# Moving a data-dependent branch forward in a mixture-of-experts block, and loading half of the last down weights by rows

## The chip, the cores and the metric

The kernel runs on one core of a Trainium2 chip. The metric is the device time in microseconds of one execution, as the median of several runs. The core has a matrix engine (TensorE, PE in the rows; its weight loads are PEld), a vector engine (VectorE, DVE), an activation engine (ScalarE, ACT), GpSimd (POOL) and SyncE (SP), which here issues nearly all DMA transfers. Each engine works through its own queue in order.

## The reference

One transformer block over 256 tokens of width 2048, in float32: RMS norm, an input projection, eight heads of a gated delta rule and eight heads of block attention, an output projection, and then a hierarchical mixture of experts with a final RMS norm. The part around the change is this one:

```python
def hierarchical_moe(x, w_rg, b_rg, w_re, b_re, w_gate, w_up, w_down):
    # 4 groups of 8 experts; each token takes the best group and the two best experts in it
    ...
    expert_id = g_idx * EXPERTS_PER_GROUP + e_idx
    y = grouped_expert_ffn(xf, expert_id, w_gate, w_up, w_down)
    out = jnp.einsum('nk,nkd->nd', gates, y.astype(jnp.float32))

# per expert, on the tokens sent to it:
#   h = silu(x @ w_gate[e]) * (x @ w_up[e]);  y = h @ w_down[e]

def reference(...):
    ...
        x = x + hierarchical_moe(h, ...)
    return rmsnorm(x, norm_final_w)
```

There are 32 experts; gate and up weights are 2048 x 512, down weights 512 x 2048, all float32, so an expert has 12.6 MB.

## The kernel before, in words

**Slots.** Every expert gets 64 slots for tokens. Experts are worked in groups of four (`quad(g, last)`, g = 0 to 7, called quads in the code), and a group in two pairs (`pr`). A pair's two experts stand side by side in the 128 partitions, 64 slots each. `one_hots` makes the tile `oh` that says which token goes to which slot; `gather` multiplies the tokens (split into a high and a low part, `xh` and `xl`) by it on TensorE into `ph`, and VectorE turns that into `hT`. `hidden` multiplies `hT` by gate and up weights (`pgate`, `pup`, 2048 rows in two halves). ScalarE and VectorE form `hg`, TensorE transposes it (`pht`) to `hgT`, and the down products go to `py`. `split_y` splits those into a high and a low part on ScalarE and VectorE (`yh`, `yl`), and `combine` adds them to the tokens: two matmuls for each half of the tokens (`pcm`) and an add on VectorE into `acc`.

**Overfull experts.** When an expert gets more than 64 tokens, `overflow` works through all tokens for it in a loop. The number of such experts is known on the device only, so there is a branch: `tc.If(n < 1)` runs the rest of the groups, and its other side runs `overflow` and then the same rest. Nothing inside the branch can be interleaved with what is outside. Before, the branch stands ahead of the last group; group 7's tokens are gathered behind it, while those of groups 1 to 6 are gathered by the group ahead.

**Loads.** `quad_loads(g)` is the list of a group's weight loads, and SP runs through these lists ahead of the other engines, held only by the ring of slots (`wslot`: nine slots of 2 MB, named `wx`, `we`, `wm`). `fetch` loads a pair's block with contiguous runs per partition. The down weights of groups 0 to 6 come by rows (256 rows of all 2048 columns at a time). Those of the last group come by columns: `LASTS` lists the blocks (pair, first column, columns), most of 512 columns for a pair of experts, in four DMA pieces each, with runs of 2 KB (1 KB for the last two).

**The tail.** In the last group the order is written out by hand (`manual_schedule`). For each block of `LASTS` TensorE makes the products (`pyl`), ScalarE and VectorE split them, and the block before is combined. `norm_part` squares the sums on ScalarE as columns become final (those of the second pair), the first 1024 columns are multiplied by the final weights `fnb` on VectorE ahead of time, and after the last column the norm's factor `rf` is worked out, the outputs are scaled and five stores go out.

Of the kernel before, what the change touches and what calls it, by code (L numbers as in the profile page):

```python
# [12 lines left out]
AF = mybir.ActivationFunctionType  # L13
# [15 lines left out]
NX, NA = 2, 5  # L29
FIRST = "x" * NX + "a" * NA + "mrm"  # L30
ROUND = "x" * NX + "a" * NA + "mm"
NQ = NE // 4
PFI, PF0 = 3, 1
XA, XB = 2, 4
WARM = (7, 2, 2)
HT = 4

LASTS = ((0, 0, 512), (1, 0, 512), (0, 512, 512), (1, 512, 512), (0, 1024, 512), (1, 1024, 512), (0, 1536, 512),
         (1, 1536, 256), (1, 1792, 256))
BS = 128 * 128 + 128  # L40


# [5 lines left out]
def tile_block(ctx, tc, x, norm_mix_w, w_in, conv_w, A_log, dt_bias, gonw, monw, w_out, nfw,  # L48
# [868 lines left out]
    def next_kind():  # L917
        used[0] += 1
        return next(kind_from(used[0] - 1))

    def wslot(kind):

        if kind == "r":
            return raw_tiles(4)
        if kind == "x":
            if len(wx["x"]) < 2 * NX:
                ts = [xtp.tile([128, 2048], F32, name="wx", tag="xw", bufs=2 * NX) for _ in range(2)]
            else:
                ts = wx["x"][-2 * NX:][:2]
            wx["x"] += ts  # L930
        elif kind == "a":
            if len(wx["e"]) < NA:
                ts = [wx["a"].tile([128, 4096], F32, name="we", tag="we", bufs=NA)]
            else:
                ts = wx["e"][-NA:][:1]
            wx["e"] += ts
        else:
            ts = [wxm.tile([128, 4096], F32, name="wm", tag="wm", bufs=2)]
        return [t.rearrange("p (k c) -> p k c", c=512) for t in ts]
# [23 lines left out]
    def quad_loads(g):  # L963

        es = range(4 * g, 4 * g + 4)
        for half in range(2):
            for w in (w_g, w_u):
                for es2 in (es[:2], es[2:]):
                    yield from fetch([w[0, e, half * 1024:(half + 1) * 1024, :].rearrange("(p k) c -> p k c", k=8)
                                      for e in es2])  # L970
        if g == NQ - 1:
            rooms = {}
            for pr, c0, n in LASTS:
                if c0 % 1024 == 0:
                    ks = [next_kind() for _ in range(2)]
                    yield ks[0]
                    rooms[pr] = [wslot(k) for k in ks]

                vs = [[t.rearrange("p k c -> p (k c)").rearrange("p (f c) -> p f c", c=1024)[:, :, c0 % 1024:c0 % 1024 + n]
                       for t in ts] for ts in rooms[pr]]  # L980
                rows = [[v[f // (4 // len(v))][:, f % (4 // len(v)):][:, 0:2] for f in (0, 2)] for v in vs]
                for i in range(2):
                    for j in range(2):
                        src = w_d[0, es[2 * pr + j], i * 256:(i + 1) * 256, c0:c0 + n]
                        nc.sync.dma_start(rows[j][i], src.rearrange("(f p) c -> p f c", p=128))
                yield [[r[f // 2][:, f % 2] for f in range(4)] for r in rows]
            return
        for es2 in (es[:2], es[2:]):
            for half in range(2):
                yield from fetch([w_d[0, e, half * 256:(half + 1) * 256, :]  # L990
                                  .rearrange("(p k) c -> p k c", k=2).rearrange("p k (i c) -> p (k i) c", c=512)
                                  for e in es2])

    gen = [0, quad_loads(0)]
    asked = [next(gen[1])]
# [13 lines left out]
    def weights():  # L1009

        while not ready:
            load_step()
        return ready.pop(0)
# [269 lines left out]
    def quad(g, last):  # L1283
# [34 lines left out]
        for pr in range(2):  # L1318
            hg = ep.tile([128, 512], F32, name="hg")
            nc.scalar.activation(hg, pgu[pr][0], AF.Silu, scale=sl[pr][:, 0:1])  # L1320
            nc.vector.scalar_tensor_tensor(hg, pgu[pr][1], sl[pr][:, 0:1], hg, op0=OP.mult, op1=OP.mult)  # L1321
            pht = ps_tmp("pht")
            for f in range(4):
                f0 = f // 2 * 256 + f % 2
                nc.tensor.transpose(pht[:, f * 128:(f + 1) * 128],
                                    hg[:, f * 128:f * 128 + 128] if last else hg[:, f0:f0 + 255:2], ident)
            hgT.append(ep.tile([128, 4, 128], F32, name="hgT", bufs=2))
            nc.scalar.copy(hgT[pr].rearrange("p f s -> p (f s)"), pht)  # L1328
        if not last and g < NQ - 2:
            noh = one_hots(g + 1)  # L1330
            nhT = [gather(noh, 0, h) for h in range(4)]
        if g == 0:
# [17 lines left out]
                if then:  # L1350
                    then(b, c0, n, pc)

        for pr in range(0 if last else 2):
            py = [ps_proj(f"py{c}") for c in range(4)]
            for f in range(4):
                if f % 2 == 0:
                    ws = weights()
                for c in range(4):
                    for j in range(2):
                        nc.tensor.matmul(py[c][j * SL:(j + 1) * SL], hgT[pr][:, f, j * SL:(j + 1) * SL],  # L1360
                                         ws[j][f % 2 * 4 + c], start=(f == 0), stop=(f == 3))
            for c in range(4):
                combine(pr, c * 512, 512, split_y(pr, 512, py[c]))
        if not last:
            if g < NQ - 2:
                start.append((noh, nhT, None))
            return

# [4 lines left out]
            nc.gpsimd.partition_broadcast(fnb[c], fnb[c][0:1], channels=128)  # L1373
        fixed = ExitStack()
        fixed.enter_context(tc.manual_schedule())
        parts_ = [(pr, c0 + o, min(n, 512), o) for pr, c0, n in LASTS for o in range(0, n, 512)]
        sums = [p for p in parts_ if p[0]]
        sf = cst.tile([128, 2, len(sums)], F32, name="sf")
        rf = cst.tile([128, 2], F32, name="rf")
        pre_ = cst.tile([128, 2], F32, name="pre_")  # L1380
        fn = lambda c0, n: fnb[c0 // 512][:, c0 % 512:c0 % 512 + n]
        late_cols = [p[1] for p in sums[-2:]]

        def norm_part(b, c0, n, pc):
            i = [p[1] for p in sums].index(c0)
            if b and c0 == late_cols[-1]:
                nc.vector.scalar_tensor_tensor(pc[:, 0:n], acc(b, c0, n), 1.0, acc(b, c0, n), op0=OP.mult, op1=OP.mult,
                                               accum_out=sf[:, b, i:i + 1])
            else:
                nc.scalar.activation(pc[:, 0:n], acc(b, c0, n), AF.Square, accum_out=sf[:, b, i:i + 1])  # L1390
                if c0 == late_cols[-1]:
                    nc.vector.scalar_tensor_tensor(pre_, sf[:, :, i - 1], 1.0 / D, pre_, op0=OP.mult, op1=OP.add)
            if c0 not in late_cols:
                if c0 < 1024:
                    muls.append((acc(b, c0, n), fn(c0, n)))

        held, muls = None, []
        for pr, c0, n, o in parts_:
            old = len(muls)
            if o == 0:  # L1400
                ws = weights()
            py = ps_proj("pyl")
            for f in range(4):
                for j in range(2):
                    nc.tensor.matmul(py[j * SL:(j + 1) * SL, 0:n], hgT[pr][:, f, j * SL:(j + 1) * SL], ws[j][f][:, o:o + n],  # L1405
                                     start=(f == 0), stop=(f == 3))
            if c0 == late_cols[-1]:
                y = ep.tile([128, 512], F32, name="hg")[:, 0:n]
                nc.scalar.activation(y, py[:, 0:n], AF.Copy, scale=sl[pr][:, 1:2])
                ys = (y,)  # L1410

                nc.vector.reduce_sum(pre_, sf[:, :, 0:len(sums) - 2], axis=AX.X)
                nc.vector.tensor_scalar(pre_, pre_, 1.0 / D, EPS, op0=OP.mult, op1=OP.add)
            else:
                ys = split_y(pr, n, py)
            if held:
                combine(*held)

            for _ in range(old):
                a, f = muls.pop(0)  # L1420
                nc.vector.tensor_mul(a, a, f)
            held = (pr, c0, n, ys, norm_part if pr else None)
        combine(*held)
        assert not muls
        ov_ = out.rearrange("o (b p) d -> (o p) b d", p=128)
        for b in range(2):
# [16 lines left out]
                nc.sync.dma_start(ov_[:, b, qs[0] * 512:qs[0] * 512 + n], a)  # L1443
        fixed.close()

    def last_quad(noh):
        start.append((noh, [gather(noh, 0, h) for h in range(4)], None))
        quad(NQ - 1, True)

    for g in range(NQ - 1):  # L1450
        quad(g, False)

    noh = one_hots(NQ - 1)
    n = nc.values_load(novi, min_val=0, max_val=7)
    seen = used[0], len(wx["x"]), list(gen), len(wx["e"])
    with tc.If(n < 1) as some:
        last_quad(noh)
    with some.Else():
        used[0], gen[:] = seen[0], seen[2]
        del wx["x"][seen[1]:]  # L1460
        del wx["e"][seen[3]:]
        overflow(n, noh)
        asked[0] = None
        last_quad(noh)


# [28 lines left out]
```

## Time and profile before

| what | value |
|---|---|
| median of 3 runs | 1430.91 us (1430.38 to 1435.44) |
| profiled execution, its own time | 1437.39 us |
| span of the profile | 1435.7 us |
| TensorE matmul busy | 1386.0 us (97%) |
| VectorE busy | 619.1 us (43%) |
| ScalarE busy | 417.0 us (29%) |
| read from device memory | 484.98 MB, 341 GB/s over the span |

A busy TensorE in this profile is not TensorE at its peak, since ends of matmuls are modelled. Each float32 matmul stands there as two instructions. The profiled execution is 6.5 us above the median of the runs.

### The profile page before, as it was taken

How to read it: one execution, taken by the hardware profiler on the slowest of the kernel's cores; microseconds unless marked ns; L12 is line 12 of the kernel's file. 1: busy time of each engine (PE TensorE's matmuls, PEld its weight loads, DVE VectorE, ACT ScalarE, POOL GpSimd, SP SyncE). 2: the span in 40 equal slices, each digit the busy share in tenths (PEclk: the TensorE clock that was granted, in tenths of full speed). 3: DMA queues.
4: the chain of work that ended last, by engine and by line, in shares of the span. 5: the costliest groups of instructions: out<-in, count | busy, mean ns of one | idle time of the engine just before them, and what ended most of it. 6: DMA issues, size and time to landing. Idle time of an engine off the chain costs nothing.

```text
span 1435.7 us, 19018 instructions
## 1 busy us (share of the span) xinstructions
PE 1386.0 (97%) x7482; PEld 815.7 (57%) x7482; DVE 619.1 (43%) x1301; ACT 417.0 (29%) x801; POOL 48.3 (3%) x84
## 2 busy tenths in 40 slices
PE   8999999999999999999999999999999899899996
PEld 8988999998888743443443443433443244235333
DVE  6876967686655541341331341241142033125014
ACT  5565436555654321120120120121121012013012
POOL 2020003000000000000000000000000000000010
PEclk9999989999999999999999999999999999999998
DMA  8667736755499689999999999999999999999996
GB/s 244 180 187 213 207 107 179 191 147 179 150 354 375 236 306 411 425 425 427 425 418 425 427 428 425 427 426 426 428 426 426 427 424 428 426 427 426 426 395 232
DMA packets 107455, 490.24 MB, mean 341 GB/s; under 512 B 23024, under 2 KB 31280, under 8 KB 78816
## 3 DMA queue, kind: packets, MB, share of 16 engines
q1 hardware_dynamic: 107056, 488.76, 87.4%
q8 instruction: 61, 1.00, 0.3%
q0 software_dynamic: 304, 0.20, 0.1%
q14 instruction: 34, 0.28, 0.1%
HBM read 484.98 MB, written 3.95 MB: 341 GB/s over the span
## 4 chain that ended last, share of the span: by engine, by line
PE 80%; DMA 10%; DVE 5%; ACT 3%; issue 1%; POOL 0%; DVEq 0%; SPq 0%; ACTq 0%
PE py L1360 15%; PE pup L1094 12%; PE pgate L1094 12%; PE pj L235 6%; PE pj L239 5%; PE pj L236 5%; DMA we<-in_w_expert_up_dram 4%; PE pj L247 4%; PE pj L248 4%; PE pj L250 4%; PE pcm L1347 3%; PE ph L1083 3%; PE pyl L1405 2%; DMA wm<-in_w_expert_up_dram 2%; DMA we<-in_w_expert_down_dram 2%; DVE acc L1349 2%
## 5 line engine op out<-in xcount | busy, mean ns | idle before, releaser
L216 DVE TENSOR_TENSOR w_lo<-w_raw,w_hi 128x512 fp32r<-128x512 f32 x288 | 193.0, 689 | 97.9 <-ACT w_hi L213 97.3
L213 ACT CAST w_hi<-w_raw 128x512 fp32r<-128x512 f32 x288 | 170.9, 619 | 84.7 <-PE pj L236 32.7
L1094 PE MATMUL pup<-we,hT 128*64 128x512 f32 x608 | 163.7, 599 | 7.7 <-DMA we<-in_w_expert_up_dram 7.6
L235 PE MATMUL pj<-xth,w_hi 128*128 128x256 f32 x640 | 168.1, 295 | 0.0
L236 PE MATMUL pj<-xtl,w_hi 128*128 128x256 f32 x640 | 161.0, 284 | 0.0
L1094 PE MATMUL pgate<-we,hT 128*64 128x512 f32 x528 | 149.3, 595 | 0.2 <-DMA we<-in_w_expert_gate_dram 0.2
L1360 PE MATMUL py<-we,hgT 128*64 128x512 f32 x480 | 144.5, 597 | 1.1 <-ACT hgT L1328 0.7
L235 PEld LDWEIGHTS pj<-xth,w_hi 128*128 128x128 f32 x640 | 122.8, 192 | 2.0 <-ACT w_hi L213 0.4
L236 PEld LDWEIGHTS pj<-xtl,w_hi 128*128 128x128 f32 x640 | 123.0, 192 | 0.3
L1072 DVE TENSOR_TENSOR hT<-ph,nfe 128x512 f32<-128x512 f32 x64 | 44.1, 688 | 169.6 <-PE pup L1094 131.7
L1321 DVE SCALAR_TENSOR_TENSOR hg<-pup,sl,hg 128x512 f32<-128x512 f32 x16 | 12.0, 751 | 231.5 <-PE pup L1094 223.6
L1338 DVE SCALAR_TENSOR_TENSOR yl<-py,sl,yh 128x512 fp32r<-128x512 f32 x56 | 40.3, 745 | 157.8 <-ACT yh L1337 156.7
L1094 PEld LDWEIGHTS pup<-we,hT 128*64 128x64 f32 x608 | 53.2, 138 | 96.7 <-issue 85.5
L1337 ACT ACTIVATE yh<-py,sl 128x512 fp32r<-128x512 f32 x56 | 37.7, 687 | 238.0 <-PE py L1360 211.9
L239 PE MATMUL pj<-xth,w_lo 128*128 128x256 f32 x640 | 103.3, 284 | 0.0
L1022 ACT CAST xh<-xs 128x512 fp32r<-128x512 f32 x64 | 73.7, 1184 | 94.3 <-PE ph L1083 64.0
L1023 DVE TENSOR_TENSOR xl<-xs,xh 128x512 fp32r<-128x512 f32 x64 | 70.6, 1118 | 47.7 <-PE ph L1083 28.7
L1094 PEld LDWEIGHTS pgate<-we,hT 128*64 128x64 f32 x528 | 45.4, 137 | 79.7 <-issue 76.2
L239 PEld LDWEIGHTS pj<-xth,w_lo 128*128 128x128 f32 x640 | 88.6, 192 | 0.0
L1349 DVE TENSOR_TENSOR acc<-acc,pcm 128x512 f32<-128x512 f32 (+1 forms) x122 | 75.4, 673 | 22.9 <-PE pcm L1347 22.8
L1360 PEld LDWEIGHTS py<-we,hgT 128*64 128x64 f32 x480 | 45.9, 136 | 66.8 <-issue 63.6
L1094 PE MATMUL pgate<-wm,hT 128*64 128x512 f32 x256 | 81.1, 595 | 0.0
(344 smaller groups left out, 1997.1 us busy)
## 6 DMA issues: line engine op xcount, KB each, us to landing
we<-in_w_expert_up_dram SPq DMA_DIRECT2D x36, 2048.0 KB, 26.9
we<-in_w_expert_gate_dram SPq DMA_DIRECT2D x33, 2048.0 KB, 24.0
we<-in_w_expert_down_dram SPq DMA_DIRECT2D x30, 2048.0 KB, 29.3
w_raw<-in_w_in_dram SPq DMA_DIRECT2D x111, 512.0 KB, 4.1
wm<-in_w_expert_gate_dram SPq DMA_DIRECT2D x16, 2048.0 KB, 28.7
wx<-in_w_expert_down_dram SPq DMA_DIRECT2D x28, 1024.0 KB, 29.4
wx<-in_w_expert_up_dram SPq DMA_DIRECT2D x28, 1024.0 KB, 26.1
wx<-in_w_expert_gate_dram SPq DMA_DIRECT2D x24, 1024.0 KB, 25.9
```

The lines of the kernel that those rows point to most:

```text
L213: nc.scalar.copy(hi, raws[n])
L216: nc.vector.tensor_sub(lo, raws.pop(n), hi.bitcast(F32))
L235: nc.tensor.matmul(o, wh[:, cs], xh[k], start=(k == 0 and c % 2 == 0), stop=False, skip_group_check=True)
L236: nc.tensor.matmul(o, wh[:, cs], xl[k], start=False, stop=False, skip_group_check=True)
L239: nc.tensor.matmul(o, wl[:, cs], xh[k], start=False, stop=(k == NK - 1), skip_group_check=True)
L247: nc.tensor.matmul(pb[b], ah[:, bs], wh, start=(k == 0), stop=False)
L248: nc.tensor.matmul(pb[b], al[:, bs], wh, start=False, stop=False)
L1022: nc.scalar.copy(hi, src)
L1023: low = lambda: nc.vector.tensor_sub(lo, src, hi.bitcast(F32))
L1094: nc.tensor.matmul(pgu[j * SL:(j + 1) * SL], hT[:, i, c0:c0 + SL], ws[j][kk], start=(half + kk == 0), stop=(half == 1 and kk == 7))
L1349: nc.vector.tensor_add(acc(b, c0, n), acc(b, c0, n) if g + pr else xs[:, b, c0:c0 + n], pc[:, 0:n])
L1360: nc.tensor.matmul(py[c][j * SL:(j + 1) * SL], hgT[pr][:, f, j * SL:(j + 1) * SL], ws[j][f % 2 * 4 + c], start=(f == 0), stop=(f == 3))
```

## The change

The branch moves from ahead of group 7 to ahead of group 4 (`BRANCH = 4`): groups 0 to 3 stand before it, groups 4 to 7 inside. The tile `oh` of the first group inside is made inside. Groups 5, 6 and 7 are gathered by the group ahead; group 4 is gathered behind the branch. In the last group the first pair's down weights are loaded by rows, as in the groups ahead, and only the second pair's by columns, in blocks of 1024, 512, 256 and 256. The hand-written order of the tail changes with it: `down(0)` makes all products of the first pair, and the products, splits and combines of the second pair's five column parts (`products`, `rows`, `add`; parts 0 to 4) are interleaved with the first pair's combines.

```diff
-NQ = NE // 4
+NQ, BRANCH = NE // 4, 4
-LASTS = ((0, 0, 512), (1, 0, 512), (0, 512, 512), (1, 512, 512), (0, 1024, 512), (1, 1024, 512), (0, 1536, 512),
-         (1, 1536, 256), (1, 1792, 256))
+LASTS = ((0, 1024), (1024, 512), (1536, 256), (1792, 256))
...
-        for es2 in (es[:2], es[2:]):
+        for es2 in (es[:2], es[2:])[:1 if g == NQ - 1 else 2]:
             for half in range(2):
                 yield from fetch([w_d[0, e, half * 256:(half + 1) * 256, :]
                                   .rearrange("(p k) c -> p k c", k=2).rearrange("p k (i c) -> p (k i) c", c=512)
                                   for e in es2])
+        if g == NQ - 1:
+            for c0, n in LASTS:
+                if c0 % 1024 == 0:
+                    ks = [next_kind() for _ in range(2)]
+                    yield ks[0]
+                    rooms = [wslot(k) for k in ks]
...
+                        src = w_d[0, es[2 + j], i * 256:(i + 1) * 256, c0:c0 + n]
+                        nc.sync.dma_start(rows[j][i], src.rearrange("(f p) c -> p f c", p=128))
...
-        if not last and g < NQ - 2:
+        if not last and g != BRANCH - 1:
             noh = one_hots(g + 1)
             nhT = [gather(noh, 0, h) for h in range(4)]
...
+        def products(i):
+            c0, n, o = sums[i]
             if o == 0:
-                ws = weights()
-            py = ps_proj("pyl")
+                blk[0] = weights()
+            pys[i] = ps_proj("pyl") if i else ps_tmp("pyl")
             for f in range(4):
                 for j in range(2):
...
+        py = down(0)
+        for i in range(2):
+            products(i)
+            ys = [split_y(0, 512, py[c]) for c in (2 * i, 2 * i + 1)]
+            for c in range(2):
+                combine(0, (2 * i + c) * 512, 512, ys[c])
+        rows(0)
+        products(2)
+        rows(1)
+        add(0)
+        rows(2)
+        products(3)
+        add(1)
+        add(2)
+        rows(3)
+        products(4)
+        rows(4)
+        add(3)
+        add(4)
...
-    def last_quad(noh):
+    def rest(noh):
         start.append((noh, [gather(noh, 0, h) for h in range(4)], None))
-        quad(NQ - 1, True)
-
-    for g in range(NQ - 1):
+        for g in range(BRANCH, NQ):
+            quad(g, g == NQ - 1)
+
+    for g in range(BRANCH):
         quad(g, False)
 
-    noh = one_hots(NQ - 1)
     n = nc.values_load(novi, min_val=0, max_val=7)
     seen = used[0], len(wx["x"]), list(gen), len(wx["e"])
     with tc.If(n < 1) as some:
-        last_quad(noh)
+        rest(one_hots(BRANCH))
     with some.Else():
...
+        noh = one_hots(BRANCH)
         overflow(n, noh)
         asked[0] = None
-        last_quad(noh)
+        rest(noh)
```

## Rows read from the trace of the kernel before

**Rows 1.** The page's 40 slices of 35.9 us: GB/s moved by DMA.
```profile
GB/s 244 180 187 213 207 107 179 191 147 179 150 354 375 236 306 411 425 425 427 425 418 425 427 428 425 427 426 426 428 426 426 427 424 428 426 427 426 426 395 232
```

**Rows 2.** Windows: us, busy PE, PEld, DVE, ACT, POOL; granted clock, DMA share, GB/s.
```profile
1248.00:1250.00 2.00, 2.00 (x6) 0.48 (x6) 0.00 (x0) 0.00 (x0) 0.00 (x0) 0.50 1.00 426
...
1310.00:1320.00 10.00, 8.20 (x44) 6.69 (x43) 9.47 (x12) 6.00 (x6) 0.00 (x0) 0.83 1.00 418
...
1314.00:1316.00 2.00, 2.00 (x12) 2.00 (x12) 2.00 (x3) 1.44 (x2) 0.00 (x0) 0.58 0.96 401
```

**Rows 3.** Timeline of TensorE: start, us, instructions, [idle before and what ended it].
```profile
1247.71 8.60 PE L1094 MATMUL pup<-we,hT 128*64 128x512 f32 x32 [3.84 <-DMA we<-in_w_expert_up_dram]
...
1309.44 0.72 PE L1083 MATMUL ph<-oh,xh 128*128 128x256 f32 x4 [0.28 <-issue]
1311.83 0.89 PE L1083 MATMUL ph<-oh,xl 128*128 128x256 f32 x4 [1.66 <-DVE xl L1023]
...
1323.41 2.79 PE L1094 MATMUL pgate<-we,hT 128*64 128x512 f32 x12
```

**Rows 4.** Timeline of SP's queue: start of an issue, its us, what it loads.
```profile
1329.68 0.33 SPq L960 DMA_DIRECT2D we<-in_w_expert_gate_dram  x1
...
1350.66 0.42 SPq L960 DMA_DIRECT2D wx<-in_w_expert_up_dram  x1
...
1413.77 0.37 SPq L985 DMA_DIRECT2D wx<-in_w_expert_down_dram  x1
```

**Rows 5.** DMA issues in windows around those three: KB, us from issue to landing.
```profile
we<-in_w_expert_gate_dram SPq DMA_DIRECT2D x1, 2048.0 KB, 17.6
...
wx<-in_w_expert_up_dram SPq DMA_DIRECT2D x1, 1024.0 KB, 26.2
...
wx<-in_w_expert_down_dram SPq DMA_DIRECT2D x1, 256.0 KB, 5.8
```

**Rows 6.** DMA packets in 1320 to 1345 us and in 1380 to 1385 us.
```profile
DMA packets 818, 10.70 MB, mean 428 GB/s; under 512 B 88, under 2 KB 88, under 8 KB 88
...
DMA packets 1054, 1.91 MB, mean 382 GB/s; under 512 B 123, under 2 KB 123, under 8 KB 1054
```

**Rows 7.** The chain that ended last, in order of time: start, us, what.
```profile
1316.55 1.21 PE ph L1083 x8
...
1366.41 6.92 PE pup L1094 x32
...
1383.46 6.20 PE pyl L1405 x26
...
1395.03 1.13 PE pcm L1347 x4
...
1411.81 3.92 PE pyl L1405 x16
...
1419.82 1.88 PE pyl L1405 x16
```

**Rows 8.** Timeline of TensorE's weight loads: the longest wait for a DMA after 1383 us.
```profile
1387.73 0.20 PEld L1405 LDWEIGHTS pyl<-we,hgT 128*64 128x64 f32 x4 [0.71 <-DMA we<-in_w_expert_down_dram]
```

**Rows 9.** Timeline of VectorE and of ScalarE in the tail.
```profile
1413.36 1.29 DVE L1421 TENSOR_TENSOR acc<-acc,fnb 128x512 f32<-128x512 f32 x2
...
1416.55 0.75 DVE L1338 SCALAR_TENSOR_TENSOR yl<-pyl,sl,yh 128x512 fp32r<-128x512 f32 x1 [1.90 <-ACT yh L1337]
1417.22 1.27 DVE L1349 TENSOR_TENSOR acc<-acc,pcm 128x512 f32<-128x512 f32 x2
...
1419.72 0.48 DVE L1338 SCALAR_TENSOR_TENSOR yl<-pyl,sl,yh 128x256 fp32r<-128x256 f32 x1 [1.23 <-ACT yh L1337]
...
1423.70 0.41 DVE L1349 TENSOR_TENSOR acc<-acc,pcm 128x256 f32<-128x256 f32 x1
...
1417.99 0.60 ACT L1390 ACTIVATE pcm<-acc 128x512 f32<-128x512 f32 x1 [1.47 <-DVE acc L1349]
...
1419.23 0.45 ACT L1337 ACTIVATE yh<-pyl,sl 128x256 fp32r<-128x256 f32 x1
```

More of the change, by code (lines that the diff above doesn't have):

```diff
@@ L970, in quad_loads @@
                                       for e in es2])
[L971 to L987, printed above, removed]
-        for es2 in (es[:2], es[2:]):
+        for es2 in (es[:2], es[2:])[:1 if g == NQ - 1 else 2]:
             for half in range(2):
@@ L992, in quad_loads @@
                                   for e in es2])
+        if g == NQ - 1:
[4 more added lines that the diff above has]
+                    rooms = [wslot(k) for k in ks]
+                vs = [[t.rearrange("p k c -> p (k c)").rearrange("p (f c) -> p f c", c=1024)[:, :, c0 % 1024:c0 % 1024 + n]
+                       for t in ts] for ts in rooms]
+                rows = [[v[f // (4 // len(v))][:, f % (4 // len(v)):][:, 0:2] for f in (0, 2)] for v in vs]
+                for i in range(2):
+                    for j in range(2):
+                        src = w_d[0, es[2 + j], i * 256:(i + 1) * 256, c0:c0 + n]
+                        nc.sync.dma_start(rows[j][i], src.rearrange("(f p) c -> p f c", p=128))
+                yield [[r[f // 2][:, f % 2] for f in range(4)] for r in rows]
     gen = [0, quad_loads(0)]
@@ L1325, in quad @@
                 nc.tensor.transpose(pht[:, f * 128:(f + 1) * 128],
-                                    hg[:, f * 128:f * 128 + 128] if last else hg[:, f0:f0 + 255:2], ident)
+                                    hg[:, f * 128:f * 128 + 128] if last and pr else hg[:, f0:f0 + 255:2], ident)
             hgT.append(ep.tile([128, 4, 128], F32, name="hgT", bufs=2))
             nc.scalar.copy(hgT[pr].rearrange("p f s -> p (f s)"), pht)
-        if not last and g < NQ - 2:
+        if not last and g != BRANCH - 1:
             noh = one_hots(g + 1)
@@ L1351, in combine, with down @@
                     then(b, c0, n, pc)
-        for pr in range(0 if last else 2):
+        def down(pr):
             py = [ps_proj(f"py{c}") for c in range(4)]
@@ L1361, in quad @@
                                          ws[j][f % 2 * 4 + c], start=(f == 0), stop=(f == 3))
-            for c in range(4):
-                combine(pr, c * 512, 512, split_y(pr, 512, py[c]))
+            return py
         if not last:
-            if g < NQ - 2:
+            for pr in range(2):
+                py = down(pr)
+                for c in range(4):
+                    combine(pr, c * 512, 512, split_y(pr, 512, py[c]))
+            if g != BRANCH - 1:
                 start.append((noh, nhT, None))
@@ L1375, in quad @@
         fixed.enter_context(tc.manual_schedule())
-        parts_ = [(pr, c0 + o, min(n, 512), o) for pr, c0, n in LASTS for o in range(0, n, 512)]
-        sums = [p for p in parts_ if p[0]]
+        sums = [(c0 + o, min(n, 512), o) for c0, n in LASTS for o in range(0, n, 512)]
         sf = cst.tile([128, 2, len(sums)], F32, name="sf")
@@ L1381, in quad @@
         fn = lambda c0, n: fnb[c0 // 512][:, c0 % 512:c0 % 512 + n]
-        late_cols = [p[1] for p in sums[-2:]]
+        late_cols = [p[0] for p in sums[-2:]]
         def norm_part(b, c0, n, pc):
-            i = [p[1] for p in sums].index(c0)
+            i = [p[0] for p in sums].index(c0)
             if b and c0 == late_cols[-1]:
@@ L1395, in norm_part, with rows @@
                     muls.append((acc(b, c0, n), fn(c0, n)))
-        held, muls = None, []
-        for pr, c0, n, o in parts_:
-            old = len(muls)
+        muls, pys, yss, blk = [], {}, {}, [None]
+        def products(i):
+            c0, n, o = sums[i]
             if o == 0:
-                ws = weights()
-            py = ps_proj("pyl")
+                blk[0] = weights()
+            pys[i] = ps_proj("pyl") if i else ps_tmp("pyl")
             for f in range(4):
                 for j in range(2):
-                    nc.tensor.matmul(py[j * SL:(j + 1) * SL, 0:n], hgT[pr][:, f, j * SL:(j + 1) * SL], ws[j][f][:, o:o + n],
-                                     start=(f == 0), stop=(f == 3))
+                    nc.tensor.matmul(pys[i][j * SL:(j + 1) * SL, 0:n], hgT[1][:, f, j * SL:(j + 1) * SL],
+                                     blk[0][j][f][:, o:o + n], start=(f == 0), stop=(f == 3))
+        def rows(i):
+            c0, n, _ = sums[i]
             if c0 == late_cols[-1]:
                 y = ep.tile([128, 512], F32, name="hg")[:, 0:n]
-                nc.scalar.activation(y, py[:, 0:n], AF.Copy, scale=sl[pr][:, 1:2])
-                ys = (y,)
+                nc.scalar.activation(y, pys[i][:, 0:n], AF.Copy, scale=sl[1][:, 1:2])
+                yss[i] = (y,)
                 nc.vector.reduce_sum(pre_, sf[:, :, 0:len(sums) - 2], axis=AX.X)
@@ L1414, in quad, with add @@
             else:
-                ys = split_y(pr, n, py)
-            if held:
-                combine(*held)
+                yss[i] = split_y(1, n, pys[i])
+        def add(i):
+            old = len(muls)
+            combine(1, *sums[i][:2], yss[i], norm_part)
             for _ in range(old):
@@ L1421, in quad @@
                 nc.vector.tensor_mul(a, a, f)
-            held = (pr, c0, n, ys, norm_part if pr else None)
-        combine(*held)
+        py = down(0)
+        for i in range(2):
+            products(i)
[15 more added lines that the diff above has]
+        add(4)
         assert not muls
```

## The prediction

> **What bounds the kernel now.** I read the slices of the page first: from about 540 us to the end of the load stream the 16 DMA engines move 411 to 428 GB/s (395 in the slice of the last columns) [rows 1], and they do so across the branch at 1310 us too, with a share of 1.00 [rows 2]. A group of four experts is 50.3 MB, so 118 us. TensorE looks as full, yet once it has caught up it waits for data: 3.84 us before 1247.71 us, for an up-projection block [rows 3]. So in the middle only bytes count, and the change loads the same bytes. What can move is the end of the stream, and the stretch from there to the last store.
>
> Next I read SP's queue beside the time to landing. The last gate/up piece is issued at 1350.66 us and lands 26.2 us later, at 1376.9; the last column piece is issued at 1413.77 and lands at 1419.6 [rows 4, 5]. So the 16.8 MB of the last down weights take 42.7 us (393 GB/s), or 5.3 us for 512 columns of an expert pair. The packets show why this is slower than before: some 13 KB each in 1320 to 1345 us at 428 GB/s, some 2 KB in 1380 to 1385 us at 382 GB/s [rows 6].
>
> Last I read the chain to the end. TensorE takes column block after column block: 3.92 us for 512 columns when it hardly waits, then 1.13 us of combining, and 1.88 us for 256 columns [rows 7]. Its waits for these pieces are short, 0.71 us the longest [rows 8]. Work and landing run level, and the last products begin at 1419.82 us, 0.2 us after the last landing. From their end at 1421.70 us it is 14 us to the end of the span.
>
> **The branch.** Before, group 7 starts behind the branch, ungathered: TensorE has idle times of 0.28 and 1.66 us, and its clean run of gate products starts only at 1323.41 us [rows 3]. The change puts this gap before group 4 (the one-hot tile is then made behind the branch too) and lets groups 5 to 7 be gathered while the group ahead still multiplies. I cost both at nothing: the cover is the queue of loads. SP, held behind the gap by slots that TensorE has not freed, issues a load at 1329.68 us, and even that one lands 17.6 us later [rows 4, 5]; so much is still queued ahead of it, and the engines never run dry [rows 2]. The ring before group 4 is the same. Behind SP's branch stand only the loads of group 4; POOL has nothing until the final norm's row. Were the cover gone, the loads would lose up to the 14 us between 1309.44 and 1323.41 us [rows 3].
>
> **Loads of the last group.** The first pair now comes by rows: 8.4 MB at 427 GB/s take 19.65 us instead of four times 5.3 = 21.2. The second pair starts with one block of 1024 columns, in 4 KB runs. No row shows 4 KB; its 4.2 MB lie between 9.8 us (427 GB/s) and 10.7 (393 GB/s), and I take 10.3, the middle. The rest keeps 5.3 us per 512 columns. So the landings go: halves of the rows at 1386.7 and 1396.5, halves of the 1024 block at 1401.7 and 1406.8, the 512 block at 1412.1, the last piece at 1417.4, 2.2 us earlier than before.
>
> By the Trainium skill (DMA: Bandwidth & Descriptors, "Why small descriptors are slow") each packet costs some 3 cycles beside its 32-byte beats, from which I work out an estimate of 420 GB/s for 4 KB, so 10.0 us and a sum 0.3 us lower. The same rule would give 410 GB/s for 2 KB, where the trace has 382 [rows 6].
>
> **TensorE on these landings.** Products by rows can't finish any column before the second half of the rows is there. The new order on TensorE is: all of the first pair's products, block 0, two combines of the first pair, block 1, the other two combines, block 2, and only then the second pair's combines. Behind each wait stand all of these, and behind them ScalarE's splits and VectorE's adds.
> - The last transposes end at 1383.5 us [rows 7]. The first row half is 16 products (32 instructions), 6.9 us at full speed [rows 7]; its second expert lands at 1386.7. That idle time is like the 3.84 us after which the granted clock fell to 0.50 and 32 such instructions took 8.60 us [rows 2, 3]; so it ends at 1395.3. The second half starts at its landing, 1396.5, and ends at 1403.4. The slow clock costs nothing here, since a landing follows.
> - Block 0: first half 1.7 us, to 1405.1; wait for 1406.8; second half and drain to 1408.9.
> - Two combines at 1.13 to 1411.2, block 1 at 3.92 to 1415.1, two combines to 1417.4, block 2 to 1421.3, combine of block 0 to 1422.4, block 3 (256 columns, 1.88) to 1424.3 [rows 7].
> - TensorE alone would go on with two combines (2.3) and block 4 (1.88), to 1428.5. Before, the last products ended at 1421.70, so this is 6.8 us later.
> - VectorE and ScalarE lag further, because block 2's split stands behind block 0's adds and squares, and block 3's behind those of blocks 1 and 2. Two adds are 1.27 us, two multiplies by the final weights 1.29, two squares 1.24; a split is 0.75 on VectorE, which I take for ScalarE too, and for 256 columns 0.45 and 0.48 [rows 9]. Block 0's adds end at 1423.2, its squares at 1423.8, block 2's split at 1425.3; adds and multiplies of block 1 and of block 2 (5.1 us) end at 1430.4; block 3's low half ends at 1430.9, the sums for the norm at 1431.2, block 3's adds at 1432.1, the last add near 1433.5. Before, it ended at 1424.1 [rows 9].
>
> Sum: +9.4 us on the last add; the 11.6 us from there to the end stay as they are. I round to +9. The profiled execution is 1437.39 us (span 1435.7) and the median of the runs 1430.91; I add the difference to the median: **1440 us**. A difference of 0.5% (7.2 us) is about what a measurement of this kernel can tell.
>
> Bounds: with 4 KB at 427 GB/s and VectorE's lag hidden, +6; with rows landing 1.5 us sooner as well, +4.5. Upward, the 1.7 us wait in block 0 may bring the slow clock again (after 1.66 us at the branch it was 0.58 [rows 2, 3]): +2; the 4 KB block at 393 GB/s +0.4; together +12, and +14 if VectorE's work collides worse.
>
> **The rivals.**
> - *The end follows the landing.* If TensorE gets through the first pair while its rows arrive and the order costs nothing, the gain of the transfers remains: 1430.9 - 2.2 = 1429, no change that can be told. For it speaks that before, TensorE ended 2 us behind the last landing; against it, that some 20 us of work (second half of block 0, three more blocks, eight combines) then lie behind the landing at 1406.8, with 10.6 us of loads to come.
> - *The gap at the branch was carried to the end* (the other side). If the late start of group 7 still made TensorE late at 1383.5, the move gives it back. The gathers themselves are 64 instructions, 9.7 us at eight in 1.21 [rows 7]; moved into group 6 they fill its 3.84 us of waiting [rows 3]. So 14 - 9.7 + 3.8 = 8.1 us, and with the transfers 10.3: 1421 us, faster. It decides once 5 us of the 8.1 reach the end. Against it: the last up weights land at 1376.9 and half a block of products, 3.4 us, hangs on them, so TensorE can't be through before 1380.3, and the transposes follow [rows 5, 7]. The Trainium skill (Runtime: NRT & Kernel Launch, "Instruction fetch mechanics") says that a taken branch breaks the prefetch of instructions and can stall an engine; by it the gap would be longer than its arithmetic, but TensorE shows 0.28 us there [rows 3].
> - *The change does not do what it says*: should group 7's gathers not move ahead, nothing changes before the tail, since the loads cover them; the forecast stands.
>
> **How the numbers follow.** Backlog as worked out, +4 to +14: 0.72, of which 0.55 is beyond +7.2 and 0.17 below it. End follows the landing, -4 to +3: 0.21. Gap given back: 0.07. So faster 0.07, same 0.38, slower 0.55. The likeliest case alone is 1435 to 1445. The range of 1428 to 1446 leaves out the faster case, part of the second and a little above, under 0.2.
>
> **What would show it.** Right: DMA share 1.0 across the branch, now near 955 us; the last landing about 2 us sooner after the gate/up weights; waits of TensorE of 3 us before the first row half and 1 to 2 us in block 0; last products 6 to 9 us later, last add 9. Wrong: no such waits because TensorE arrives late anyway; last products within 3 us of the last landing; or a hole in the DMA stream at the new branch, which would add its length.

## Result, and the profile after

The changed kernel takes 1444.12 us (median of 6 runs, 1441.60 to 1444.87), the kernel before, beside it, 1433.26 us (6 runs, 1430.38 to 1437.23). The ratio is 1.0073, 95% interval 1.0059 to 1.0087: slower by 8.5 to 12.5 us. The forecast was 1440 us against a median of 1430.91, so +9, with most of the chance on slower by over 0.5%.

The two profiled executions differ by less, 1437.39 and 1444.22 us. The one before is among that kernel's slower runs, and in the one after the load stream is already 1.6 us earlier at 540 us. So I count both from the moment **U** at which the last up weights have landed: the change to the tail lies wholly behind it, and only the moved branch lies ahead of it. U itself differs from one execution to the next: it is 1369.2 to 1378.5 us in the traces of the changed kernel and of its versions with another tail, which are the same ahead of it. So a single execution can gain or lose several us before the tail begins. Before, U is 1350.66 + 26.2 = 1376.9 us and the span ends 58.8 us later [rows 4, 5]. After, the timeline of SP's queue and the landings of its issues, in windows around the last up piece and the last column piece, say:

```profile
1347.39 0.42 SPq L959 DMA_DIRECT2D wx<-in_w_expert_up_dram  x1
...
1409.52 0.37 SPq L988 DMA_DIRECT2D wx<-in_w_expert_down_dram  x1
```

```profile
wx<-in_w_expert_up_dram SPq DMA_DIRECT2D x1, 1024.0 KB, 27.2
...
wx<-in_w_expert_down_dram SPq DMA_DIRECT2D x1, 256.0 KB, 5.8
```

U is 1374.6, the span of 1442.5 us ends 67.9 later: **+9.1 us** behind U, while the last piece lands at 1415.3, U + 40.7 instead of U + 42.7. The loads end 2 us sooner and the kernel 9 later. From the last add into `acc` to the end of the span it is 11.6 us before and 12.2 after, and 11.5 to 13.7 in the traces of the experiments, so the last add, which is 8.5 us later (below), is the steadier mark. The page's slices show the stream as before [rows 1], and the windows across the branch's new place (columns as in [rows 2]) no hole in it:

```profile
GB/s 262 163 183 212 217 100 186 190 147 179 167 343 364 219 353 412 426 421 428 426 417 426 425 427 427 427 426 425 428 426 427 425 427 426 428 425 425 427 416 117
...
940.00:950.00 10.00, 9.77 (x39) 4.23 (x35) 4.11 (x7) 2.75 (x4) 0.00 (x0) 1.00 1.00 426
950.00:960.00 10.00, 7.20 (x34) 5.71 (x34) 10.00 (x15) 5.77 (x5) 0.00 (x0) 0.83 0.99 421
960.00:970.00 10.00, 9.54 (x54) 5.85 (x56) 7.45 (x8) 5.90 (x5) 0.00 (x0) 1.00 1.03 433
```

TensorE works 7.20 of 10 us there (9.36 in the same window before), at a clock of 0.83; DMA loses nothing: 0.99 to 1.03. In the tail TensorE's timeline has the waits that the kernel before has not [rows 8]:

```profile
1384.47 7.09 PE L1357 MATMUL py<-we,hgT 128*64 128x512 f32 x32 [3.11 <-DMA we<-in_w_expert_down_dram]
1394.28 6.65 PE L1357 MATMUL py<-we,hgT 128*64 128x512 f32 x29 [2.73 <-DMA we<-in_w_expert_down_dram]
...
1404.16 1.93 PE L1406 MATMUL pyl<-wm,hgT 128*64 128x512 f32 x6 [1.07 <-DMA wm<-in_w_expert_down_dram]
...
1422.68 1.95 PE L1406 MATMUL pyl<-wx,hgT 128*64 128x256 f32 x16
...
1426.57 0.38 PE L1344 MATMUL pcm<-yh,GT 128*128 128x256 f32 x1 [1.94 <-ACT yh L1334]
```

Two waits for the row halves, one for the second half of block 0, and then none: every later block is there before TensorE comes to it. The last wait is for ScalarE's split. The chain that ended last, in order of time, names what binds at each point:

```profile
1347.39 27.19 DMA wx<-in_w_expert_up_dram
...
1374.59 29.52 DMA wm<-in_w_expert_down_dram
...
1404.16 1.93 PE pyl L1406 x6
1406.09 2.18 PE pcm L1344 x8
1408.26 3.58 PE pyl L1406 x16
1411.85 2.18 PE pcm L1344 x8
1414.03 3.58 PE pyl L1406 x16
1417.61 0.68 PE pcm L1344 x2
...
1418.32 0.70 DVE acc L1346
...
1419.04 0.62 ACT pcm L1390 x2
...
1420.37 0.58 ACT yh L1334
...
1420.98 0.75 DVE yl L1335
...
1423.13 1.00 DVE acc L1427 x2
1424.13 1.20 DVE acc L1346 x2
1425.32 1.20 DVE acc L1427 x2
...
1427.09 2.73 PE pcm L1344 x7
```

Up to 1404.1 us it is the DMA stream; then TensorE, serially, to 1418.3 us; from there VectorE and ScalarE. The split of block 2 (`yh`, `yl`) stands behind the adds and the squares (line 1390) of block 0, and the split of block 3, which TensorE's last combines need, behind two pairs of adds and of multiplies by the final weights (line 1427). The last adds:

```profile
1425.24 1.29 DVE L1427 TENSOR_TENSOR acc<-acc,fnb 128x512 f32<-128x512 f32 x2
1426.55 0.48 DVE L1335 SCALAR_TENSOR_TENSOR yl<-pyl,sl,yh 128x256 fp32r<-128x256 f32 x1
...
1429.84 0.42 DVE L1346 TENSOR_TENSOR acc<-acc,pcm 128x256 f32<-128x256 f32 x1 [0.36 <-PE pcm L1344]
```

The last products end at 1424.6, U + 50.0 (before U + 44.8), the last add at 1430.26, U + 55.7 (before U + 47.2 [rows 7, 9]). So of 8.5 us, 5.2 are there at the end of the last products, and 3.3 come behind them. About 2.0 of the 3.3 are the wait for the split. Some 1.2 more lie in the last combines: from the start of the first of them to the last add it is 2.5 us before and 3.7 after. Their start before, and a window on them after (columns as in [rows 2]):

```profile
1421.63 0.38 PE L1347 MATMUL pcm<-yh,GT 128*128 128x256 f32 x1
...
1427.00:1430.00 3.00, 2.72 (x7) 1.82 (x7) 1.76 (x8) 1.44 (x6) 0.00 (x0) 0.50 0.02 5
```

Behind that wait of 1.94 us the granted clock is 0.50, the lower of TensorE's two levels (1.2 GHz); before, without the wait, it is 1.00 to the last add. In the trace of the tail alone (below), where the clock fell about 1 us later, the same stretch is 2.9 us.

### The profile page after: what moved, and what is told of

Read it like the earlier page. It is cut to its first block, busy times and chain, and to the rows that moved or that the text cites. A ratio compares the mean times of both kernels' runs of the same rounds, so it can differ in the third digit from the quotient of the medians.

```text
span 1442.5 us, 18986 instructions
## 1 busy us (share of the span) xinstructions
PE 1385.0 (96%) x7482; PEld 812.9 (56%) x7482; DVE 619.0 (43%) x1301; ACT 416.1 (29%) x801; POOL 50.0 (3%) x84
## 4 chain that ended last, share of the span: by engine, by line
PE 78%; DMA 12%; DVE 6%; ACT 3%; issue 1%; POOL 0%; SPq 0%; DVEq 0%; ACTq 0%
PE py L1357 15%; PE pup L1091 13%; PE pgate L1091 12%; PE pj L234 6%; PE pj L238 5%; PE pj L235 5%; DMA we<-in_w_expert_up_dram 4%; PE pcm L1344 3%; PE ph L1080 3%; PE pj L246 3%; PE pj L247 3%; PE pj L249 3%; DVE acc L1346 2%; DMA wm<-in_w_expert_down_dram 2%; DMA w_raw<-in_w_out_dram 2%; DMA wx<-in_w_expert_up_dram 2%
## 5 line engine op out<-in xcount | busy, mean ns | idle before, releaser
L1357 PE MATMUL py<-we,hgT 128*64 128x512 f32 x544 | 159.6, 597 | 7.0 <-DMA we<-in_w_expert_down_dram 6.3
L1335 DVE SCALAR_TENSOR_TENSOR yl<-py,sl,yh 128x512 fp32r<-128x512 f32 x60 | 43.2, 746 | 177.6 <-ACT yh L1334 176.4
L1357 PEld LDWEIGHTS py<-we,hgT 128*64 128x64 f32 x544 | 50.3, 136 | 81.7 <-issue 71.9
L1020 DVE TENSOR_TENSOR xl<-xs,xh 128x512 fp32r<-128x512 f32 x64 | 70.7, 1119 | 40.5 <-PE ph L1080 29.8
```

Of the source, the lines that this page charges most:

```text
L1020: low = lambda: nc.vector.tensor_sub(lo, src, hi.bitcast(F32))
```

## The experiments

The theory under test: the loss is all in the tail, and a landing costs when the serial work that hangs behind it (products, combines, and the adds at VectorE's pace) is longer than the loads still to come. Rivals: the branch costs some of it; the transfers by rows cost it as such. All ratios are to the kernel before on the same chip, taken beside them (medians 1433.6 to 1434.1 us). Since those carry 2 to 4 us of uncertainty, I also give the last add's distance from U in the trace (before +47.2, after +55.7). The changed kernel itself ran beside them only in the last comparison; in the first, the nearest to it is the changed kernel with the branch moved back.

**Which part.** The kernel before with only the branch moved, and the changed kernel with only the branch moved back:

```diff
# kernel before
-        if not last and g < NQ - 2:
+        if not last and g != BRANCH - 1:
...
-        quad(NQ - 1, True)
+        for g in range(BRANCH, NQ):
+            quad(g, g == NQ - 1)
...
-    for g in range(NQ - 1):
+    for g in range(BRANCH):
# changed kernel
-NQ, BRANCH = NE // 4, 4
+NQ, BRANCH = NE // 4, 7
```

> The kernel before with the branch moved ahead of group 4 and groups 5 to 7 gathered ahead; loads and tail as before. Theory (the queue of loads covers the branch; the loss is all in the order of the tail): no change, within 2 us of the kernel before, a ratio of 0.9985 to 1.0015, DMA share 1.0 across the branch near 955 us. Rival (the branch in the middle costs part of the 10.9 us): slower by 4 us or more, a ratio of 1.003 and up.

> The changed kernel with the branch back ahead of group 7; loads and tail of the change. Theory: the whole loss is here, 9 to 11 us slower than the kernel before, a ratio of 1.006 to 1.008. Rival (the branch costs part): at most 6 us slower, a ratio below 1.0045.

Measured: the branch alone 1435.68 us, ratio 1.0009 (0.9993 to 1.0025); the tail alone 1444.25, 1.0063 (1.0046 to 1.0080); last add at U + 47.9 and U + 55.2. The tail alone shows the loss of the whole change; what the branch costs can't be told from nothing, and by the interval is 3.6 us at most. In the trace of the branch alone, the window at the new place has the clock of the changed kernel, a gap like its own, and full DMA:

```profile
950.00:960.00 10.00, 8.27 (x41) 6.42 (x41) 9.70 (x14) 5.83 (x6) 0.00 (x0) 0.83 1.00 423
```

**Transfers or work.** The changed kernel with the second half of the first pair's rows not loaded; the products use the first half twice, so the output is another. That is 4.2 MB, 9.8 us, less to load with the same work.

```diff
-            for half in range(2):
+            for half in range(1 if g == NQ - 1 else 2):
...
-                if f % 2 == 0:
+                if f == 0 or f == 2 and not last:
```

> The changed kernel without the load of the second row half of the first pair's last down weights (4.2 MB, 9.8 us of loads): its products take the first half's weights a second time. All blocks behind land 9.8 us sooner. Theory (TensorE's work behind the landings sets the end): only the waits go, 2.7 us before the second row half and 1.1 us in block 0, so 3 to 5 us faster than the changed kernel, 6 to 8 us slower than the kernel before. Rival (the end follows the last landing): 9 to 10 us faster than the changed kernel, about level with the kernel before.

Measured: 1439.18, ratio 1.0037 (1.0021 to 1.0054); last add at U + 52.4. Of 9.8 us of transfers taken away, 3.3 (by the last add) to 5.1 (against the tail alone, on the same chip) come back, and it is still slower than the kernel before, which loads all. In the chain that ended last, no transfer stands behind the first row half:

```profile
1354.21 25.87 DMA we<-in_w_expert_down_dram
...
1380.12 15.21 PE py L1357 x61
...
1410.72 0.68 PE pcm L1344 x2
```

From 1380.1 to 1411.4 us it is TensorE alone, then VectorE and ScalarE as in the changed kernel. So transfers are not what ends the changed kernel; the work behind them is. (In this trace the granted clock was 0.57 from 1380 to 1384 us; the 61 instructions took 15.2 us, against 7.09 + 6.65 in the changed kernel, so by the trace alone some 1.5 us more might have come back.)

**A finer landing.** The same rows in four alternating pieces of 1 MB an expert:

```diff
-    def fetch(srcs):
+    def fetch(srcs, parts=1):
...
-                                  for e in es2])
+                                  for e in es2], 2 if g == NQ - 1 else 1)
```

> The changed kernel with the first pair's rows loaded in quarters (1 MB pieces that alternate between the two experts) and not in halves, so that TensorE can begin 4.9 us sooner and end the first pair's products about 3.4 us sooner. Theory (what binds is the landing of block 0's second half, at 1404 us, with all the rest behind it in a fixed order): the wait only moves into block 0 and grows there from 1.1 to 4 or 5 us; within 1.5 us of the changed kernel. Rival (the waits for the row halves themselves are the price): 3 to 4 us faster than the changed kernel.

Measured: 1442.91, ratio 1.0056 (1.0034 to 1.0079), last add at U + 55.5: level with the tail alone. TensorE's weight loads show where the time went:

```profile
1392.14 0.20 PEld L1357 LDWEIGHTS py<-we,hgT 128*64 128x64 f32 x4 [1.99 <-DMA we<-in_w_expert_down_dram]
1397.03 0.20 PEld L1406 LDWEIGHTS pyl<-wm,hgT 128*64 128x64 f32 x4 [2.12 <-DMA wm<-in_w_expert_down_dram]
1399.50 0.19 PEld L1406 LDWEIGHTS pyl<-wm,hgT 128*64 128x64 f32 x2 [1.42 <-DMA wm<-in_w_expert_down_dram]
1402.00 0.20 PEld L1406 LDWEIGHTS pyl<-wm,hgT 128*64 128x64 f32 x4 [2.31 <-DMA wm<-in_w_expert_down_dram]
```

The rows are done sooner, and TensorE then waits 5.9 us inside block 0, for its halves. Its second half binds, as in the changed kernel.

**Combines into that wait.** With the quarters, all four combines of the first pair ahead of block 0:

```diff
-        for i in range(2):
-            products(i)
-            ys = [split_y(0, 512, py[c]) for c in (2 * i, 2 * i + 1)]
-            for c in range(2):
-                combine(0, (2 * i + c) * 512, 512, ys[c])
+        for c in range(4):
+            combine(0, c * 512, 512, split_y(0, 512, py[c]))
+        products(0)
+        products(1)
```

> The first pair's rows in quarters as in e4, and in the tail's order all four combines of the first pair ahead of the products of block 0, which is where e4 showed TensorE waiting 5.9 us. Theory (the wait for block 0's landing is fixed; what stands behind it sets the end): 4.4 us of combining move into the wait, about 1.2 us of them past the landing, so 3 us faster than e4, 3 to 5 us faster than the changed kernel, 5 to 7 us slower than the kernel before. Rival (the end follows the last landing, or the order does not matter): level with e4.

Measured: 1445.72, ratio 1.0072 (1.0047 to 1.0098), last add at U + 54.8. The expectation missed: the last add is 0.7 us sooner than with the quarters alone, and the time no better, which is what the rival said. I had priced the combines at TensorE's 1.1 us each. TensorE's timeline in this stretch, then VectorE's:

```profile
1400.57 0.50 PE L1344 MATMUL pcm<-yl,GT 128*128 128x512 f32 x1 [1.34 <-DVE yl L1335]
...
1403.10 0.50 PE L1344 MATMUL pcm<-yl,GT 128*128 128x512 f32 x1 [1.34 <-DVE yl L1335]
...
1406.55 1.94 PE L1406 MATMUL pyl<-wm,hgT 128*64 128x512 f32 x8
```

```profile
1401.10 1.29 DVE L1346 TENSOR_TENSOR acc<-acc,pcm 128x512 f32<-128x512 f32 x2 [0.59 <-PE pcm L1344]
1402.30 0.75 DVE L1335 SCALAR_TENSOR_TENSOR yl<-py,sl,yh 128x512 fp32r<-128x512 f32 x1
1403.64 1.28 DVE L1346 TENSOR_TENSOR acc<-acc,pcm 128x512 f32<-128x512 f32 x2 [0.59 <-PE pcm L1344]
```

With nothing between them, the combines come every 2.53 us: VectorE adds (1.29), only then splits the next columns (0.75), whose combine TensorE then makes, while VectorE waits (0.59) for it. The four take 8.7 us, from 1397.8 to 1406.5, instead of 4.4. The wait for block 0 is gone, and one for VectorE is in its place.

**VectorE's lag.** The changed kernel without the squares of columns 0 to 1535 and without the early multiplies by the final weights (both left out of the output):

```diff
-                nc.scalar.activation(pc[:, 0:n], acc(b, c0, n), AF.Square, accum_out=sf[:, b, i:i + 1])
+                if c0 in late_cols:
+                    nc.scalar.activation(pc[:, 0:n], acc(b, c0, n), AF.Square, accum_out=sf[:, b, i:i + 1])
...
-                a, f = muls.pop(0)
-                nc.vector.tensor_mul(a, a, f)
+                muls.pop(0)
```

> The changed kernel without the squares of the first 1536 columns on ScalarE and without the early multiplies by the final weights on VectorE (both left out of the result; loads, products and combines stay). Theory (a good third of the loss is that splits stand behind this work late in the tail): last add about 3.4 us sooner, 3 to 4 us faster than the changed kernel. Rival (TensorE and the landings alone set the end): within 1 us of the changed kernel.

Measured: 1440.03, ratio 1.0039 (1.0022 to 1.0056); last add at U + 52.6, 3.1 sooner than after. That agrees with the 3.3 us of lag read above, and holds both its parts: the last combines wait for no split here, and the granted clock stays at 1.00. The gain rests on the trace; the times alone would not show it, since the changed kernel did not run beside this one, and its ratios elsewhere are 1.0045 to 1.0073.

**The first pair's rows sooner.** The changed kernel with the last group's second half in the order gate and up of the first pair, gate of the second, rows of the first, up of the second, then the columns in blocks of 512; work in the same order (the edit also moves code, which is left out here):

```diff
+        if g == NQ - 1:
+            return up[:4] + [(1, 0, 0), (1, 1, 0), (1, 0, 1), (0, 2, 0), (1, 2, 0), (1, 1, 1)]
```

> From the changed kernel: in the last group the second half of the first pair's up weights and its down rows are loaded and worked ahead of the second pair's last up block, so that only the second pair's columns (blocks of 512, 512, 512, 256, 256) come behind the last up weights. Theory: the first pair's products by rows then lie where TensorE has work on both sides, and the tail runs level with the landings as before; the rows still save 1.6 us of loads: 1 to 4 us faster than the kernel before, a ratio of 0.997 to 0.9995. Rival (rows for the first pair cost as such, by waits for their halves, wherever they stand): 5 us or more slower than the kernel before.

Measured: 1441.11, ratio 1.0046 (1.0028 to 1.0064). The expectation missed again, and the number, 7.2 us slower than the kernel before, is in the range of the rival. TensorE's timeline, at the second row half and at the first column block:

```profile
1380.11 1.93 PE L1327 MATMUL py<-we,hgT 128*64 128x512 f32 x4 [1.26 <-DMA we<-in_w_expert_down_dram]
...
1402.78 3.65 PE L1419 MATMUL pyl<-wm,hgT 128*64 128x512 f32 x16 [0.68 <-ACT hgT L1300]
```

Behind the row half at 1380.1 now lie its products (7.1), four combines with VectorE between them (6.4), a block of up products (7.0), the activation and transposes, and all the columns (some 20 us): over 40 us, with 9.8 + 21 = 31 us of loads to come. The backlog was moved, not cut. The rival's reason, waits for the row halves, is not what the trace shows: TensorE waits 1.26 us for them.

**The work between.** So the work must shrink behind the landing, and combines must never follow each other closely. The second pair's 1024 block becomes two of 512, the rows come in quarters, and one combine of the first pair stands between the products of two blocks. The same with the rows in halves, and the changed kernel once more, ran beside it:

```diff
-LASTS = ((0, 1024), (1024, 512), (1536, 256), (1792, 256))
+LASTS = ((0, 512), (512, 512), (1024, 512), (1536, 256), (1792, 256))
...
+        first = [split_y(0, 512, py[c]) for c in range(2)]
+        products(0)
+        combine(0, 0, 512, first[0])
+        rows(0)
+        products(1)
+        combine(0, 512, 512, first[1])
+        first.append(split_y(0, 512, py[2]))
+        add(0)
+        rows(1)
+        products(2)
+        combine(0, 1024, 512, first[2])
...
```

> The changed kernel with the row halves in four 1 MB quarters, the second pair's first 1024 columns as two blocks of 512, and the order of the tail written anew: behind the first pair's row products, products of one column block, one combine of the first pair, products of the next block, one combine, and so on, with no more than two y tiles waiting. Same bytes, same 2 KB runs of the columns as the kernel before. Our theory (what counts is the serial work that hangs behind a landing, against the loads that are still to come; rows as such cost nothing): the work behind the second pair's first block falls by half, and the combines find their splits done, so 3 to 8 us faster than the changed kernel, 1436 to 1441 in sessions where the kernel before takes 1434. Rival (the rows themselves cost it: four accumulators finish at once after the second row half, and their combines can't run earlier whatever the order): level with the changed kernel, 1443 to 1446.

> The same new order and blocks of 512, but the rows in two halves of 2 MB each as in the changed kernel. Our theory: the row products of the second half (7 us) then start only when all of it has landed, so up to 3 us slower than with the quarters, and still 1 to 5 us faster than the changed kernel. Rival as for the quarters: level with the changed kernel.

> The changed kernel itself, as the measure for the two others on the same chip: both theories expect 8 to 12 us over the kernel before.

Measured, on one chip: with quarters 1435.94 us, ratio 1.0014 (1.0002 to 1.0025), last add at U + 50.5; with halves 1439.66, 1.0046 (1.0028 to 1.0064), U + 53.1; the changed kernel itself 1439.80, 1.0045 (1.0029 to 1.0061), U + 55.2. The changed kernel's own loss is thus 6 us here, below the 8 to 12 expected, and was 10 in the first comparison, the intervals just touching; its two traces give 67.8 us (here) and 67.9 from U to the end of the span. With quarters the new order is 3.9 us faster than the changed kernel by the medians, 4.7 by the traces, within what the theory expected. With halves the times are level with the changed kernel, as the rival said, and the gain of 2.1 us that the traces show can't be told in them. U and the last add with the quarters, from the chain that ended last:

```profile
1353.20 25.27 DMA wx<-in_w_expert_up_dram
...
1428.67 0.34 DVE acc L1346
```

TensorE's weight loads wait for the last row quarter and for two column blocks:

```profile
1399.19 0.20 PEld L1357 LDWEIGHTS py<-we,hgT 128*64 128x64 f32 x4 [2.08 <-DMA we<-in_w_expert_down_dram]
1404.21 0.32 PEld L1406 LDWEIGHTS pyl<-wm,hgT 128*64 128x64 f32 x4 [0.54 <-DMA wm<-in_w_expert_down_dram]
1409.37 0.27 PEld L1406 LDWEIGHTS pyl<-wm,hgT 128*64 128x64 f32 x3 [0.15 <-DMA wm<-in_w_expert_down_dram]
```

Waits of 0.54 and 0.15 us at the landings of columns are the picture of the kernel before [rows 8]: at these two blocks work and landing are level again. The last products end 5 us behind the last landing, against 9.3 in the changed kernel and 2.1 in the kernel before. What is left, 3.3 us at the last add, is 2.5 on TensorE (last products at U + 47.3), which still waits for row quarters, and the rest VectorE's and ScalarE's. No version beat the kernel before.

Two things are not separated. The quarters alone gave nothing, the new order and blocks without them 2.1 us in the traces, all together 4.7; the blocks of 512 under the old order were not tried. And since 3.3 us remain with the rows, a cost of that size that comes with loading by rows, whatever the order, is not ruled out.

## Why the prediction was right, step by step

- **Branch, at nothing.** Shown by itself: 1.0009 (0.9993 to 1.0025). TensorE's wait at the new place is 2.11 us for VectorE's one-hot tile and 0.51 for a split, and no load waits. The rival "gap at the branch carried to the end" asked for 5 us of gain; the branch alone gave none. By the Trainium skill (Runtime: NRT & Kernel Launch, "Instruction fetch mechanics") a taken branch can stall an engine's fetch. In the trace TensorE's idle time there waits for VectorE, which is busy all through 950 to 960 us, and no run here shows such a stall as a time.
- **Landings.** Forecast behind U: row halves +9.8 and +19.6, block 0's second half +29.9, last piece +40.5. Measured (by the products' start): +9.9, +19.7, +29.5, +40.7. The second pair's 8.4 MB took 21.0 us, forecast 20.9, but two terms were off that cancel: block 0 landed 9.83 us behind the second row half and not 10.3, and the rest took 11.2 us and not 10.6. The 9.83 us are no rate of 4 KB runs, since loads follow each other without a gap and part of block 0 moved before the rows had landed (of 625 packets between 1384.5 and 1394.3 us, 470 are under 8 KB). Between 1394 and 1398 us nearly all packets are of 4 KB, and they move at 418 GB/s (the row is in the last section). At that rate 4.2 MB take 10.0 us, inside the prediction's bounds. The Trainium skill (DMA: Bandwidth & Descriptors, "Why small descriptors are slow") gave an estimate of 420 GB/s for 4 KB. The trace agrees, with 418.
- **TensorE on them.** The idle times came where forecast: 3.11, 2.73 and 1.07 us (forecast 3.2, 1.2 and 1.7). The first row half ran at full clock in 7.09 us, where I had taken 8.60 at the low one; the end does not see it, since the next landing follows, as the prediction says. Behind block 0's landing, TensorE was quicker than its terms: 3.58 us a block, not 3.92 [rows 7], which is a block that still waits a little. Last products at U + 50.0, forecast U + 51.6: 5.2 us later than before, less than the 6 to 9 that the prediction named as a sign of being right.
- **VectorE and ScalarE.** Lag over the kernel before 3.3 us, forecast 2.6 (9.4 less 6.8). By its place it is the one forecast: splits queued behind adds, squares and multiplies, and taking squares and multiplies away gave 3.1 us. But some 1.2 of it is the low clock of the last combines, a term that the forecast did not have there.
- **Sum.** Last add +8.5 us against U, forecast +9.4; from there to the end of the span 0.6 more than before. That the sum is this near is partly luck: TensorE came out 1.6 us sooner than forecast, and the lag behind it 0.7 longer. My 9.4 was counted from the profiled execution and put on the median; the traces' +9.1 and the medians' +10.9 (8.5 to 12.5) both allow it. The 1444.12 us themselves are 13 above the 1430.91 that the forecast stood on, since the kernel before took 1433.26 beside them.
- **The rival "end follows the landing"** fell on the point named against it: with the landing at U + 29.5, 20.5 us pass to the end of the last products and 26.2 to the last add, with 11.2 us of loads to come. Removing 9.8 us of loads gave back about half at most.

What stays open: why the ratio of the same kernel is 1.0073 in one comparison and 1.0045 in another, with the same tail in both traces. The traces show that executions of kernels that are the same ahead of U can have U 9 us apart; why is not known.

## What to carry to other kernels

At every landing near the end, set the serial work that hangs on it (at the pace of the whole loop between the engines, here 2.5 us a combine when a split waits for the adds ahead of it in VectorE's queue, not TensorE's 1.1) against the loads still to come. Here columns that finish at once kept the two level, and rows that finish nothing until the last piece piled the work up behind it. A faster transfer gains little once the work behind it is the longer of the two: 2 us sooner gained nothing, and 9.8 us gave 3 to 5. A data-dependent gap can lie where queued loads cover it: moving it cost nothing that these runs can tell, with the DMA engines at a share of 0.99 to 1.03 across its new place.

## What the runs showed of the hardware that was not expected

The 4 KB runs moved at 418 GB/s, close to the 425 to 428 of most slices of the stream before them, the 2 KB runs of the kernel before at 382 to 397. DMA packets of the changed kernel from 1394 to 1398 us:

```profile
DMA packets 439, 1.67 MB, mean 418 GB/s; under 512 B 28, under 2 KB 28, under 8 KB 439
```

And the same wait of 3.1 us ahead of the same row products was followed by a lower granted clock in some executions and not in others. Windows of 8 us around the first row half, in the changed kernel, in its later run, and in the new order with halves:

```profile
1384.00:1392.00 8.00, 7.09 (x32) 2.21 (x32) 0.00 (x0) 0.00 (x0) 2.20 (x5) 1.00 1.00 418
```

```profile
1384.00:1392.00 8.00, 8.00 (x26) 2.26 (x24) 0.00 (x0) 0.00 (x0) 2.25 (x4) 0.67 0.99 411
```

```profile
1378.00:1386.00 8.00, 6.90 (x20) 2.10 (x22) 0.00 (x0) 0.00 (x0) 2.77 (x5) 0.57 1.00 416
```

At a granted clock of 1.00 the 32 instructions took 7.09 us; in the last of these executions, partly at 0.50, the lower of the two levels, 9.95. The last add behind U was not later for it (55.2 against 55.7 us in the second and first), because the next row half had still to land. A shorter wait, the 1.94 us ahead of the changed kernel's last combines, was followed by 0.50 as well, and there nothing covered it.
